# First SwiGLU with six hidden blocks at once and stationary weights in two parts; attention bias stored by 32 keys

## The chip, the cores and the metric

The program runs on one core of one Trainium2 chip. The metric is the device time of one execution in microseconds (us); lower is better. Beside a time there is the span of a profiled execution, which runs from its first to its last instruction and is a little shorter than the time. Five engines matter: PE (TensorE, matrix products), DVE (VectorE), ACT (ScalarE), POOL (GpSimd) and SP (SyncE, which here does nothing but issue transfers). On chip there are SBUF, 128 partitions wide, and PSUM, where PE accumulates. Weights come from DRAM by DMA.

## The reference

Two transformer layers on x of 256 tokens by D = 1024, all in fp32. A layer is: a SwiGLU, an attention, a second SwiGLU, each behind an RMS norm and a modulation by shift, scale and gate that are computed from a vector c.

```python
c_act = jax.nn.silu(c)
for layer in range(2):
    mods = c_act @ ada_w[layer] + ada_b[layer]
    sh1, sc1, g1, sh2, sc2, g2, sh3, sc3, g3 = jnp.split(mods, 9, axis=-1)
    h = modulate(rms_norm(x, norm_g[layer, 0]), sh1, sc1)       # h * (1 + scale) + shift
    x = x + 0.5 * g1 * swiglu(h, w_gate, w_up, w_down)          # (silu(h wg) * (h wu)) wd, F = 2816
    h = modulate(rms_norm(x, norm_g[layer, 1]), sh2, sc2)
    mix = moba_attention(h, ..., rel_bias, positions) if layer == 0 else mla_attention(h, ...)
    x = x + g2 * mix
    ...                                                         # second SwiGLU, as the first
```

The attention of layer 0 has 16 heads of 64 and adds to its scores a bias that depends on the distance of query and key: `bias_t[h, t5_bucket(qpos - kpos)]`, with 32 buckets, and minus a large number for keys that come after the query.

## The kernel before

**Products in parts.** Nearly all matrix products are made in a split form. An fp32 tile is rounded to a high part (ACT, line 623, `hi`) and the rest is its low part (DVE, line 624, `lo`); both are of a type that PE takes at a higher rate. `mm3` (lines 751 to 754) then adds up three products: high by high, low by high, high by low. `split_evac` (line 766) does the same to a result in PSUM, with `hh`/`hl` for activations.

**Order.** The program is written down in one order, and then a planner (`Order`, lines 238 on) lists all instructions of each engine anew. It costs every instruction with hand-set durations (`duration`, line 195), takes the PE order and the needs of later work as due times, and picks for each engine the most urgent one that is ready. `ranked(j)` gives the instructions of the first stage fixed ranks that override the due times; `hold` marks the bias and table work as side work that may not begin before the planned time `HELD`. Tiles come from rings of a fixed number of buffers, and a transfer into a buffer waits until the last reader of the tile before it is done. SP issues its transfers in order.

**The first SwiGLU.** It needs `h`, the normed and modulated x, before the modulation's vectors exist. So `first()` (line 1450) works through the eight slices `k` of 128 along D. For each slice: two column tiles `wt[k][0..1]` (128 x 1024) arrive, DVE multiplies each with c and sums along the row (`column`, line 634, one custom instruction and a short read of the accumulator), and `scale_col` (line 639) makes the scale out of it. x times 1/rms (line 1500, on ACT, with 1/rms from a small POOL operation, line 789) is transposed on PE (line 1502, "tr<-ident,y"). DVE makes z = xT * scale + shift (line 1510). Then come unsplit fp32 products: z is stationary, the 2 x 512 columns of the gate and up weights move (line 1514, two token tiles, four products a slice, 32 in all; in the trace one such product has two records). They make the first 512 of the 2816 hidden columns, with tokens along the partitions. z is split into the `hh`/`hl` that all later products use. The result, `accs`, goes through Silu (ACT) and a product (DVE, line 892), is transposed back (eight transposes of 128 x 128) and split.

**The rest of that SwiGLU** runs in pairs of blocks of 128 hidden columns (loop over `f0` in steps of 256, from line 905; "block n" is hidden columns 128n to 128n + 127). Here the weights are stationary and `h` moves: for each block 2 x 8 `mm3` of 256 columns (48 products), then the Silu (line 925, "g<-mm"), the product with the up part (line 926) and a split. The weights come as 1 MB loads of 128 x 2048 (`raw`, three buffers), and are split in two pieces of 1024. At the same time DVE works on the modulation vectors of later parts: columns as above, and accumulations (line 672, "acc<-adaw,cols,acc"), which "adaps" products (lines 682 and 683) sum up.

**The bias** is side work in the same loop. `bias_steps` (line 1078) makes comparisons on DVE (line 1149, "oh<-posq,key": 64 of them, in eight tiles `oh` of eight, four 256 wide and four 128 wide), and groups of 24 short bf16 products on PE (line 1128, "tr<-tab,oh", twelve groups), which turn the comparisons into bias values. After `k` of `HOOKS` of each block one group is put into the order, and all are in before `f0` = `SIDE_TO` * 256. ACT copies each group in four pieces into `bt` (line 1133; one tile of 128 x 2048 per pair of query tile and key tile). Two of the three `bt` are masked by a POOL affine select (line 1137), and all three are written to DRAM, `bias_d`, in four transfers each with 512 bytes in a run. The attention of layer 0 reads `bias_d` back in four groups of four heads on POOL's queue (line 1178, 6 KB in a run), and DVE adds it to the scores as it takes their minimum (line 989, "s<-at,bg"). `rope_tables` and `mla_consts` (among them line 1308, short products on DVE) are further side work, let in from `f0` = `ROPE_AT` * 256.

Of the kernel before, what the change touches and what calls it, by code (L numbers as in the profile page):

```python
# [21 lines left out]
P = 128  # L22
# [6 lines left out]
FB = 512  # L29
H = 16  # L30
DH = 64
GH = 4
# [22 lines left out]
SIDE_TO = 4  # L55
ROPE_AT = 7
# [29 lines left out]
def weight_tiles():  # L86


    for layer in range(2):
        for idx in range(2):  # L90
# [5 lines left out]
            for f0 in range(FB, F, S):  # L96
                for w in (wg, wu):
                    yield [(*w, f0)], 0, KD, S
# [27 lines left out]
def lay_out(v):  # L126
# [11 lines left out]
    out["first"] = np.stack([v["ffn_w_" + n][0, 0, :, :FB].reshape(KD, P, FB) for n in ("gate", "up")], axis=2)  # L138
# [23 lines left out]
    keys = pos.view(np.float32).reshape(NT, 4, 1, NB).repeat(NB, axis=2).reshape(NT, P, NB)  # L162
# [20 lines left out]
HELD = 34e3  # L183
# [334 lines left out]
def trunk(ctx: ExitStack, tc: tile.TileContext, a: dict, out: bass.AP):  # L518
# [351 lines left out]
    def ffn(layer, idx, h, after, ada_to, start=None):  # L870

        last = (layer, idx) == (1, 1)
        with ExitStack() as st:
            gp = st.enter_context(tc.tile_pool(name=nm("gp"), bufs=1))
            gT = {}
            accs = start() if start else {t: [] for t in range(NT)}
            ada_pace(ada_to, 90.0 if last else FFN_PACE)
            parts = [] if start else [[], []]
            for t in range(NT):
# [24 lines left out]
            gq = gp  # L904
            for f0 in range(FB, F, S):
# [8 lines left out]
                for f in range(f0 // P, (f0 + S) // P):  # L914
# [9 lines left out]
                    g = gp.tile([P, NT, P], F32, tag="gT", name=nm("g"), bufs=2)  # L924
                    nc.scalar.activation(g, ps[:, 0], AF.Silu)  # L925
                    nc.vector.tensor_tensor(g, ps[:, 1], g, op=ALU.mult)  # L926
                    gh, gl = [gq.tile([P, NT, P], F32R, tag=f"{nme}{f}", name=nm(nme)) for nme in ("gh", "gl")]
                    split_evac(gh, gl, g)
                    for t in range(NT):
                        gT[f, t] = gh[:, t, :], gl[:, t, :]  # L930
# [28 lines left out]
    def attention(ap, g, qTs, kTs, vs, bias, oT, state, after_s=None):  # L959
# [6 lines left out]
        def scores():  # L966
# [14 lines left out]
            for (t, es), ps3 in zip(UNITS, banks):  # L981
# [5 lines left out]
                else:  # L987
                    for i, e in enumerate(es):
                        nc.vector.tensor_tensor_reduce(s3[:, i, :], ps3[:, i, :], bias(t, e), 1.0, 3.0e38,
                                                       op0=ALU.add, op1=ALU.min, accum_out=mx[:, i:i + 1])  # L990
# [81 lines left out]
    bias_d = dp.tile([NG, P, GH * 3 * P], F32, name="bias_d")  # L1072
# [5 lines left out]
    def bias_steps():  # L1078
# [5 lines left out]
        with ExitStack() as st:  # L1084
# [35 lines left out]
            bt = {}  # L1120

            def mms(kb, t, c, oh):
                if c == 0:
                    bt[kb, t] = bp.tile([P, H, P], F32, tag="bt", name=nm("bt"), bufs=2)
# [6 lines left out]
                dst = bt[kb, t].rearrange("p h (j i) -> p h j i", j=4)  # L1131
                for j in range(4):
                    nc.scalar.activation(dst[:, :, j, 8 * c:8 * c + 8],
                         pt.rearrange("p (i j h) -> p j h i", i=8, j=4)[:, j], AF.Copy)
                if c == 3:
                    if t == kb:
                        nc.gpsimd.affine_select(bt[kb, t], bt[kb, t], pattern=[[0, H], [-1, P]],
                                                compare_op=ALU.is_ge, fill=-NEG, base=0, channel_multiplier=1)
                    for g in range(NG):
                        nc.sync.dma_start(  # L1140
                            bias_d[g].rearrange("p (h k) -> p h k", h=GH)[:, :, (t + kb) * P:(t + kb + 1) * P],
                            bt[kb, t][:, g * GH:(g + 1) * GH, :])

            for kb in range(NT):
                n = P * (NT - kb)
                for c in range(4):
                    oh = bp.tile([P, 8, n], BF16, tag="oh", name=nm("oh"), bufs=2)
# [26 lines left out]
    def moba(h, after):  # L1174
        with ExitStack() as st:
            ap = st.enter_context(tc.tile_pool(name="moba", bufs=1))
            bg = {0: ap.tile([P, GH, 3 * P], F32, tag="bg", name=nm("bg"))}
            nc.gpsimd.dma_start(bg[0].rearrange("p h k -> p (h k)"), bias_d[0])
# [42 lines left out]
            def to_T(g):  # L1221
# [16 lines left out]
                def load_bias():  # L1238
                    if g + 1 < NG:
                        bg[g + 1] = ap.tile([P, GH, 3 * P], F32, tag="bg", name=nm("bg"))  # L1240
# [108 lines left out]
    def mla(h, hs, after):  # L1349
        with ExitStack() as st:  # L1350
# [96 lines left out]
            out_proj(oT, (1, 1), after)  # L1447


    def first():  # L1450


        key = (0, 0)
# [113 lines left out]
```

## Time and profile before

| | before |
|---|---|
| time, median of 3 runs | 1019.33 us (1019.13 to 1019.91) |
| time of the profiled execution | 1019.3 us |
| its span | 1017.5 us |
| granted TensorE clock, mean | 1.000 |
| read from DRAM, written | 255.34 MB, 4.19 MB |
| unsplit products of the first stage, busy time up to 106 us | 23.1 us in 48 records and 7.1 us in 16 |
| high parts on ACT (all) | 325.5 us in 316, mean 1041 ns |
| low parts on DVE (all) | 375.2 us in 316, mean 1201 ns |
| copies of the bias on ACT | 9.3 us in 48, mean 298 ns |

How to read the profile's lines. The first part of the page gives for each engine its busy time, the share of the span and the number of instructions; PEld is the loading of stationary tiles, which overlaps PE. Products are pipelined: one that is listed with 0.28 us may have another start 0.12 us after it. A line of the timeline gives start and duration in us, engine, line of the code, operation, tiles (out<-in), shape and type, "xN" for N in a row put together, and in brackets the idle time ahead of it with what ended it. A table of windows has one row for each stretch of time: its length, and then for each engine the busy time with the number of instructions. The chain of waits is followed back from the last instruction: at each step to what released it.

### The profile page before, as it was taken

What the parts mean: (1) busy time and instruction counts of PE and PEld (TensorE: products, weight loads), DVE (VectorE), ACT (ScalarE), POOL (GpSimd) and SP (SyncE); (2) the same over time, 40 slices, a digit from 0 to 9 for tenths busy, and PEclk for the clock granted to TensorE, in tenths of its full rate; (3) what the DMA queues carried; (4) which work ended last, traced back from release to release, by engine and by line L of the source; (5) the groups of instructions that cost most, each with busy time, mean ns of one, the idle gap of its engine ahead of it and who ended that gap; (6) DMA issues with size and microseconds to landing.
All of it is one profiled execution on the core that took longest, in us unless ns stands there. A gap on an engine that the chain in (4) does not pass through costs nothing.

```text
span 1017.5 us, 16904 instructions
## 1 busy us (share of the span) xinstructions
PE 1000.0 (98%) x6538; PEld 885.5 (87%) x6538; DVE 805.9 (79%) x1310; ACT 566.7 (56%) x1008; POOL 76.7 (8%) x118
## 2 busy tenths in 40 slices
PE   7999999999999999999999999999999999999998
PEld 3598998888888799999888999988888889999986
DVE  7999888799989899888889986544998789555542
ACT  4354544368757774455357445543779785455421
POOL 2011000012231000000000000000143010000000
PEclk9999999999999999999999999999999999999999
DMA  9969999889885689988988995463343467544530
GB/s 361 412 227 341 324 338 325 307 302 345 293 327 189 244 302 369 325 316 309 350 313 319 342 333 179 166 227 106 104 138 131 173 229 276 200 167 166 211 141 21
DMA packets 56578, 260.63 MB, mean 256 GB/s; under 512 B 6065, under 2 KB 12721, under 8 KB 38066
## 3 DMA queue, kind: packets, MB, share of 16 engines
q1 hardware_dynamic: 55442, 256.05, 69.6%
q0 software_dynamic: 768, 3.17, 0.9%
q8 instruction: 51, 0.84, 0.3%
q10 hardware_dynamic: 288, 0.33, 0.2%
q14 instruction: 29, 0.24, 0.1%
HBM read 255.34 MB, written 4.19 MB: 255 GB/s over the span
## 4 chain that ended last, share of the span: by engine, by line
PE 88%; DVE 7%; DMA 3%; ACT 1%; issue 1%; POOL 0%; SPq 0%; ACTq 0%; DVEq 0%
PE mm L752 26%; PE mm L754 26%; PE mm L753 26%; PE mm L1514 2%; PE at L976 2%; DVE oh L1149 1%; DVE lo L624 1%; PE at L1031 1%; DMA btab<-in_tab_dram 1%; PE at L1011 1%; PE tr L802 1%; DVE acc L672 1%; DMA bias_d<-bt 1%; DMA raw<-in_w_dram 1%; DMA x<-in_x_dram 0%
## 5 line engine op out<-in xcount | busy, mean ns | idle before, releaser
L624 DVE TENSOR_TENSOR lo<-raw,hi 128x1024 fp32r<-128x1024 f32 (+2 forms) x316 | 375.2, 1201 | 117.6 <-ACT hi L623 117.1
L623 ACT ACTIVATE hi<-raw 128x1024 fp32r<-128x1024 f32 (+2 forms) x316 | 325.5, 1041 | 174.3 <-PE mm L754 121.9
L752 PE MATMUL mm<-hh,hi 128*128 128x256 f32 x1152 | 323.6, 284 | 0.7 <-ACT hi L623 0.7
L754 PE MATMUL mm<-hh,lo 128*128 128x256 f32 x1152 | 322.9, 283 | 0.7 <-DVE lo L624 0.7
L753 PE MATMUL mm<-hl,hi 128*128 128x256 f32 x1152 | 322.9, 283 | 0.0
L752 PEld LDWEIGHTS mm<-hh,hi 128*128 128x128 f32 x1152 | 219.3, 192 | 1.9 <-ACT hi L623 0.9
L754 PEld LDWEIGHTS mm<-hh,lo 128*128 128x128 f32 x1152 | 219.7, 192 | 1.4 <-DVE lo L624 0.9
L753 PEld LDWEIGHTS mm<-hl,hi 128*128 128x128 f32 x1152 | 220.0, 192 | 0.9 <-issue 0.2
L634 DVE CUSTOM_DVE_ANT_0 adaw<-adaw,c_b,cols 128x1024 f32<-128x1024 f32 x112 | 141.3, 1282 | 3.3 <-DMA adaw<-in_ada_dram 2.9
L752 PE MATMUL mm<-hi,gh 128*128 128x512 f32 x352 | 137.1, 390 | 0.0
L753 PE MATMUL mm<-lo,gh 128*128 128x512 f32 x352 | 136.8, 389 | 0.0
L754 PE MATMUL mm<-hi,gl 128*128 128x512 f32 x352 | 136.6, 389 | 0.0
L925 ACT ACTIVATE g<-mm 128x256 f32<-128x256 f32 x72 | 27.6, 383 | 139.2 <-PE mm L754 123.8
L752 PE MATMUL mm<-hi,hh 128*128 128x512 f32 (+1 forms) x240 | 95.2, 402 | 0.6 <-ACT hh L767 0.5
L754 PE MATMUL mm<-hi,hl 128*128 128x512 f32 (+1 forms) x240 | 92.5, 392 | 1.6 <-DVE hl L768 1.6
L753 PE MATMUL mm<-lo,hh 128*128 128x512 f32 (+1 forms) x240 | 93.3, 393 | 0.0
L754 PEld LDWEIGHTS mm<-hi,gl 128*128 128x128 f32 x352 | 66.1, 188 | 13.7
L753 PEld LDWEIGHTS mm<-lo,gh 128*128 128x128 f32 x352 | 66.1, 188 | 13.3
L752 PEld LDWEIGHTS mm<-hi,gh 128*128 128x128 f32 x352 | 66.1, 188 | 13.2
L672 DVE SCALAR_TENSOR_TENSOR acc<-adaw,cols,acc 128x1024 f32<-128x1024 f32 x48 | 61.3, 1278 | 0.1
L926 DVE TENSOR_TENSOR g<-mm,g 128x256 f32<-128x256 f32 x72 | 30.3, 421 | 34.9 <-ACT g L925 34.7
L754 PEld LDWEIGHTS mm<-hi,hl 128*128 128x128 f32 x240 | 45.1, 188 | 10.5 <-DVE hl L768 2.1
(204 smaller groups left out, 1081.8 us busy)
## 6 DMA issues: line engine op xcount, KB each, us to landing
raw<-in_w_dram SPq DMA_DIRECT2D x144, 1024.0 KB, 6.2
adaw<-in_ada_dram SPq DMA_DIRECT2D x160, 512.0 KB, 6.3
raw<-in_w_dram SPq DMA_DIRECT2D x12, 512.0 KB, 3.7
raw<-in_w_dram SPq DMA_DIRECT2D x6, 576.0 KB, 3.6
raw<-in_first_dram SPq DMA_DIRECT2D x6, 512.0 KB, 10.2
bias_d<-bt SPq DMA_DIRECT2D x12, 256.0 KB, 5.6
bg<-bias_d POOLq DMA_DIRECT2D x4, 768.0 KB, 5.6
raw<-in_w_dram SPq DMA_DIRECT2D x2, 768.0 KB, 4.3
```

What stands on the lines that cost most here:

```text
L623: nc.scalar.activation(hi, src, AF.Copy)
L624: nc.vector.tensor_tensor(lo, src, hi.bitcast(F32), op=ALU.subtract)
L634: nc.vector.tensor_tensor_reduce(wt, wt, c_b, 1.0, cols[:, i, c:c + 1], op0=ALU.mult, op1=ALU.add, accum_out=m_cols[:, i, c:c + 1])
L672: nc.vector.scalar_tensor_tensor(acc, ada_tile(j, k), cact[:, k:k + 1], acc, op0=ALU.mult, op1=ALU.add)
L752: nc.tensor.matmul(ps, lh, rh, start=start, stop=False)
L753: nc.tensor.matmul(ps, lh, rl, start=False, stop=False)
L754: nc.tensor.matmul(ps, ll, rh, start=False, stop=stop)
L802: nc.tensor.transpose(kslice(pt, j), kslice(y, j), ident)
L925: nc.scalar.activation(g, ps[:, 0], AF.Silu)
L926: nc.vector.tensor_tensor(g, ps[:, 1], g, op=ALU.mult)
L976: nc.tensor.matmul(ps3[:, i, :], qTs(e, t), kTs(e, nk), start=bias is not None, stop=bias is not None or i == len(es) - 1)
L1514: nc.tensor.matmul(accs[t][i], kslice(z, t), w1[k][:, i * FB:(i + 1) * FB], start=k == 0, stop=k == KD - 1)
```

## The change

Eight things are changed, all in the first SwiGLU and in the bias of layer 0's attention.

- `first` makes six blocks (`B1` = 6, 768 hidden columns) in place of the first four. The weights are now stationary, in high and low parts, and `h` moves, as in the rest of the loop: 8 slices x 6 blocks x 2 matrices x 3 products of 256 columns. All six blocks accumulate side by side in six PSUM banks, each with gate and up in one bank. So no result needs transposing, and each goes through `units`, the code that the other blocks use. The loop over `f0` starts at 768.
- Since two accumulations share a bank, each bank is first cleared by products with a tile of zeros (nine of them, bf16, 512 columns, before any data is there).
- x is transposed by a product with a diagonal matrix that holds 1/rms: x is stationary, `diag[t]` moves (16 fp32 products). This replaces the scaling on ACT, the transposes and the copy of `xT` to SBUF. Ten short products with zeros follow those of slice 1.
- z is made on ACT, from PSUM, and no longer on DVE.
- The weights of a slice are 128 x 1536: the high parts in three ACT copies of 512; of the low part, DVE and POOL do one half each (512 + 256 columns and 256 + 512) for slices 0 to 5, and DVE does all of it for slices 6 and 7.
- These weights come in 24 transfers of 256 KB (with six slices' worth of buffers, three of `raw` and three of `adaw`), in place of eight of 512 KB.
- The bias is kept by 32 keys: each group of 24 products gives one `bt` tile (128 x 16 heads x 32 keys), by one ACT copy; eight of the twelve are masked, by an affine select of 512 each; each is written by one transfer with 2 KB in a run. It is read back with 512 bytes in a run, and DVE reads scores and bias with a four-dimensional pattern. The order of the keys in the table of key positions is changed accordingly. `oh` has three buffers, `bt` three.
- `SIDE_TO` goes from 4 to 6, `ROPE_AT` from 7 to 9, `HELD` from 34e3 to 40e3 (planned ns).

The core of the diff:

```diff
-SIDE_TO = 4
-ROPE_AT = 7
+B1 = 6
+SIDE_TO = 6
+ROPE_AT = 9
...
-HELD = 34e3
+HELD = 40e3
...
-    out["first"] = np.stack([v["ffn_w_" + n][0, 0, :, :FB].reshape(KD, P, FB) for n in ("gate", "up")], axis=2)
+    out["first"] = np.stack([v["ffn_w_" + n][0, 0, :, :B1 * P].reshape(KD, P, B1, P) for n in ("gate", "up")], axis=3)
+    out["first"] = out["first"].reshape(KD, P, 3, -1).transpose(0, 2, 1, 3)
...
+            def units(f, ps):
+                g = gp.tile([P, NT, P], F32, tag="gT", name=nm("g"), bufs=2)
+                nc.scalar.activation(g, ps[:, 0], AF.Silu)
+                nc.vector.tensor_tensor(g, ps[:, 1], g, op=ALU.mult)
+                gh, gl = [gq.tile([P, NT, P], F32R, tag=f"{nme}{f}", name=nm(nme)) for nme in ("gh", "gl")]
+                split_evac(gh, gl, g)
...
-            for f0 in range(FB, F, S):
+            for f0 in range(B1 * P if start else FB, F, S):
...
-    bias_d = dp.tile([NG, P, GH * 3 * P], F32, name="bias_d")
+    bias_d = dp.tile([3, P // NB, P, H * NB], F32, name="bias_d")
...
-                dst = bt[kb, t].rearrange("p h (j i) -> p h j i", j=4)
-                for j in range(4):
-                    nc.scalar.activation(dst[:, :, j, 8 * c:8 * c + 8],
-                         pt.rearrange("p (i j h) -> p j h i", i=8, j=4)[:, j], AF.Copy)
-                if c == 3:
-                    if t == kb:
-                        nc.gpsimd.affine_select(bt[kb, t], bt[kb, t], pattern=[[0, H], [-1, P]],
-                                                compare_op=ALU.is_ge, fill=-NEG, base=0, channel_multiplier=1)
-                    for g in range(NG):
-                        nc.sync.dma_start(
-                            bias_d[g].rearrange("p (h k) -> p h k", h=GH)[:, :, (t + kb) * P:(t + kb + 1) * P],
-                            bt[kb, t][:, g * GH:(g + 1) * GH, :])
+                bt = bp.tile([P, H, NB], F32, tag="bt", name=nm("bt"), bufs=3)
+                nc.scalar.activation(bt, pt.rearrange("p (m h) -> p h m", h=H), AF.Copy)
+                if t == kb:
+                    nc.gpsimd.affine_select(bt, bt, pattern=[[0, H], [-1, NB]], compare_op=ALU.is_ge, fill=-NEG,
+                                            base=-NB * c, channel_multiplier=1)
+                nc.sync.dma_start(bias_d[t + kb, c], bt.rearrange("p h k -> p (h k)"))
...
+            def load_bias(g):
+                bg[g] = ap.tile([P, 3, P // NB, GH * NB], F32, tag="bg", name=nm("bg"))
+                cs = slice(g * GH * NB, (g + 1) * GH * NB)
+                nc.gpsimd.dma_start(bg[g], bias_d[:, :, :, cs].rearrange("u c p f -> p u c f"))
...
+            for f in (*range(B1), *range(3)):
+                nc.tensor.matmul(accs[f], zeros[:, :P], zeros, start=f not in cleared, stop=False)
+                cleared.add(f)
...
+                    diag.append(fp.tile([P, P], F32, name=nm("diag")))
+                    nc.scalar.activation(diag[t], ident, AF.Copy, scale=rstd_of(t))
...
+            def transposed(k):
+                xT = ps_x[k % 2][:, :S]
+                with ranked(2 * k + 1):
+                    for t in range(NT):
+                        nc.tensor.matmul(kslice(xT, t), kslice(xs[t], k), diag[t], start=True, stop=k != 1 or t == 0)
+                    for i in range(fill if k == 1 else 0):
+                        nc.tensor.matmul(kslice(xT, 1), zeros[:, :P], zeros[:, :P], start=False, stop=i == fill - 1)
+                return xT
...
                     for i in range(2):
                         column(key, i, k, wt[k][i])
                     scale_col(key, k, 1)
                     z = tp.tile([P, S], F32, tag="y", name=nm("z"), bufs=4)
-                nc.vector.tensor_scalar(z, xT[k // 4][:, k % 4 * S:(k % 4 + 1) * S], col_slice(1, key, k, 1), col_slice(0, key, k, 1),
-                                        op0=ALU.mult, op1=ALU.add)
+                    nc.scalar.activation(z, xT[k], AF.Identity, scale=key, k, 1), bias=col_slice(0, key, k, 1))
...
-                for i in range(2):
-                    nc.tensor.matmul(accs[t][i], kslice(z, t), w1[k][:, i * FB:(i + 1) * FB],
-                                     start=k == 0, stop=k == KD - 1)
+                    hi, lo = [fp.tile([P, n1], F32R, tag=g, name=nm(g), bufs=2) for g in ("whi", "wlo")]
+                    for j in range(3):
+                        cs = slice(j * third, (j + 1) * third)
+                        nc.scalar.activation(hi[:, cs], w1(k, j), AF.Copy)
+                        cut = (0, third // 2, third)[j] if k < KD - 2 else 0
+                        for on, c0, c1 in ((nc.vector, 0, third - cut), (nc.gpsimd, third - cut, third)):
+                            if c0 < c1:
+                                on.tensor_tensor(lo[:, j * third + c0:j * third + c1], w1(k, j)[:, c0:c1],
+                                                 hi.bitcast(F32)[:, j * third + c0:j * third + c1], op=ALU.subtract)
...
+                for f in range(B1):
+                    for i in range(2):
+                        c = (2 * f + i) * P
+                        ps, wh, wl = accs[f][:, i], hi[:, c:c + P], lo[:, c:c + P]
+                        nc.tensor.matmul(ps, wh, hh, start=False, stop=False)
+                        nc.tensor.matmul(ps, wh, hl, start=False, stop=False)
+                        nc.tensor.matmul(ps, wl, hh, start=False, stop=i == 1 and k == KD - 1)
...
+            for f in range(B1):
+                units(f, accs[f])
```

168 lines of the change are left out of this document (84 added, 84 removed).

## The prediction

> **What bounds the kernel now.** I read the page's busy table and chain first, then the windows of the first 120 us, since everything the change touches ends there or (the bias) is read by 330 us.
>
> ```profile
> PE 1000.0 (98%) x6538; PEld 885.5 (87%) x6538; DVE 805.9 (79%) x1310; ACT 566.7 (56%) x1008; POOL 76.7 (8%) x118
> ...
> PE 88%; DVE 7%; DMA 3%; ACT 1%; issue 1%; POOL 0%; SPq 0%; ACTq 0%; DVEq 0%
> ...
> 20.00:30.00 10.00, 10.00 (x24) 4.37 (x23) 9.01 (x17) 0.84 (x2) 0.00 (x0) 1.00 1.03 410
> ...
> 60.00:80.00 20.00, 18.97 (x292) 18.23 (x291) 20.00 (x52) 9.83 (x30) 3.60 (x1) 1.00 0.76 249
> 80.00:100.00 20.00, 18.40 (x167) 17.66 (x166) 19.80 (x33) 11.43 (x29) 3.84 (x3) 1.00 1.04 347
> 100.00:120.00 20.00, 20.00 (x167) 19.91 (x166) 17.58 (x28) 10.83 (x18) 0.00 (x0) 1.00 0.95 352
> ```
>
> The columns are PE, PEld, DVE, ACT, POOL, clock, DMA share, GB/s. PE bounds the whole, but between 60 and 100 us DVE is full (20.00 and 19.80 of 20) and PE is not. Before that DMA is full (1.03). So the early stage has three limits in turn, and a gain of PE time there counts only if DVE follows. From 100 us PE is full and DVE has 12% spare: what PE has gained by then stays gained.
>
> The stage on PE, in order of time:
>
> ```profile
> 10.32 1.97 PE L1502 MATMUL tr<-ident,y 128*128 128x128 f32 x8 [0.28 <-ACT y L1500]
> ...
> 13.63 23.06 PE L1514 MATMUL mm<-raw,z 128*128 128x512 f32 x48
> 36.88 7.11 PE L1514 MATMUL mm<-w,z 128*128 128x512 f32 x16 [0.18 <-DMA w<-in_first_dram]
> ...
> 43.94 0.28 PE L753 MATMUL mm<-hl,hi 128*128 128x256 f32 x1
> 44.06 0.28 PE L754 MATMUL mm<-hh,lo 128*128 128x256 f32 x1
> ...
> 55.48 0.87 PE L1128 MATMUL tr<-tab,oh 128*128 128x64 bf16 x24
> 56.19 0.36 PE L752 MATMUL mm<-hh,hi 128*128 128x256 f32 x1
> ...
> 97.18 0.39 PE L682 MATMUL adaps<-hi,ones_r 128*128 128x512 f32 x1
> 97.41 0.40 PE L683 MATMUL adaps<-lo,ones_r 128*128 128x512 f32 x1
> ...
> 106.19 0.39 ACT L925 ACTIVATE g<-mm 128x256 f32<-128x256 f32 x1 [0.59 <-PE mm L754]
> ```
>
> The f32 matmuls hold PE from 13.63 to 43.4 us. After that a split matmul of 256 columns starts every 0.12 us, and a bias group of 24 costs 0.71 us. My milestone is the last row: the Silu of block 11 (the first 1536 of the 2816 hidden columns and all bias groups done), at 106.2 us.
>
> **The change on PE.** Removed: the f32 matmuls (29.8 us as they ran), 96 split matmuls of blocks 4 and 5 (11.5), eight transposes. Added: 6 blocks x 2 matrices x 3 x 8 = 288 split matmuls, 288 x 0.12 = 34.6 us, and 16 products with the diagonal. Nothing like the latter stands in the trace; the transposes above cost 1.97/8 = 0.25 us, an f32 512-column record about 23.06/48 = 0.48, so 0.12 to 0.25; I take 0.25, of which 12 fall after the start: 3 us. The nine clearing matmuls resemble the 0.23 us of the adaps rows, lie ahead of the first data, and cost the path 0 to 0.5. Starting at 13.6 as now, PE alone would finish six blocks at 51.2 and, with 6 x 48 x 0.12 = 34.6 and 12 groups of 0.79 (0.71 and a slower restart), reach the milestone at 95.3. The four adaps matmuls (0.9 us), now ahead of it, come later in the changed order, so like stands against 105.3: PE alone gains about 10 us.
>
> **The change on DVE.** DVE's own costs, from rows that follow one another without a gap:
>
> ```profile
> 8.21 1.28 DVE L634 CUSTOM_DVE_ANT_0 adaw<-adaw,c_b,cols 128x1024 f32<-128x1024 f32 x1 [0.36 <-ACT y L1500]
> ...
> 16.26 1.28 DVE L634 CUSTOM_DVE_ANT_0 adaw<-adaw,c_b,cols 128x1024 f32<-128x1024 f32 x1 [0.52 <-DMA adaw<-in_ada_dram]
> 18.75 0.15 DVE L639 SCALAR_TENSOR_TENSOR m_cols<-m_cols,cols 128x1 f32<-128x1 f32 x1
> ...
> 20.10 1.28 DVE L634 CUSTOM_DVE_ANT_0 adaw<-adaw,c_b,cols 128x1024 f32<-128x1024 f32 x1 [0.34 <-DMA adaw<-in_ada_dram]
> ...
> 42.77 0.68 DVE L892 TENSOR_TENSOR g<-mm,g 128x512 f32<-128x512 f32 x1
> 43.37 1.22 DVE L624 TENSOR_TENSOR lo<-raw,hi 128x1024 fp32r<-128x1024 f32 x1
> ...
> 62.71 2.19 DVE L1149 TENSOR_SCALAR oh<-posq,key 128x256 bf16<-128x256 f32 x8
> 64.81 1.22 DVE L624 TENSOR_TENSOR lo<-raw,hi 128x1024 fp32r<-128x1024 f32 x1
> 65.94 0.42 DVE L926 TENSOR_TENSOR g<-mm,g 128x256 f32<-128x256 f32 x1
> 66.28 1.22 DVE L624 TENSOR_TENSOR lo<-raw,hi 128x1024 fp32r<-128x1024 f32 x1
> 67.41 1.66 DVE L1149 TENSOR_SCALAR oh<-posq,key 128x128 bf16<-128x128 f32 x8
> 68.98 0.42 DVE L926 TENSOR_TENSOR g<-mm,g 128x256 f32<-128x256 f32 x1
> 69.31 1.28 DVE L672 SCALAR_TENSOR_TENSOR acc<-adaw,cols,acc 128x1024 f32<-128x1024 f32 x1
> 70.51 1.22 DVE L624 TENSOR_TENSOR lo<-raw,hi 128x1024 fp32r<-128x1024 f32 x1
> 71.64 2.00 DVE L1308 TENSOR_TENSOR sink<-rw_sin,cols 128x16 f32<-128x16 f32 x1
> 73.57 1.65 DVE L1149 TENSOR_SCALAR oh<-posq,key 128x128 bf16<-128x128 f32 x8
> ...
> 86.00 1.98 DVE L1308 TENSOR_TENSOR sink<-rw_sin,cols 128x16 f32<-128x16 f32 x1
> 87.91 0.16 DVE L1308 TENSOR_TENSOR cosq<-rw_cos,cols 128x16 f32<-128x16 f32 x1
> ```
>
> From start to start: two columns 2.49 us, with the scaling 2.64; a difference over 512 columns 0.60, over 1024 1.13, over 256 0.34; a comparison 0.26 (256 wide) or 0.20 (128); an accumulation 1.20. In the first stage the changed DVE does 8 x 2.64 = 21.1, eight low parts of z 2.7, and low parts of the weights: 6 x (0.60 + 0.34) for k below 6, and 6 x 0.60 for the last two, 9.2. Sum 33.0; the z products go to ACT, which is busy 56%. Beginning at 8.2 as now, with some 1.5 us of waits (the second pair of columns waits for its load, low parts of z wait for ACT, both estimated), it would end at 42.7. DMA does not hold that up: the pairs now come 3.84 us apart for 1.5 MB, so 4.5 us for 1.75 MB.
>
> But POOL now does the other 768 low columns of each k below 6, and here is the crux:
>
> ```profile
> 70.02 3.60 POOL L1137 TENSOR_SCALAR_AFFINE_SELECT bt<-bt 128x2048 f32<-128x2048 f32 x1 [57.85 <-ACT bt L1133]
> ...
> 85.61 2.34 POOL L1137 TENSOR_SCALAR_AFFINE_SELECT bt<-bt 128x2048 f32<-128x2048 f32 x1 [11.99 <-DMA bias_d<-bt]
> ```
>
> Both times a 16-element DVE product beside it took 2.00 and 1.98 us in place of 0.16, until POOL's end; the first select had itself waited through two DVE instructions. They exclude each other, and POOL holds DVE about 1.85 us for 2048 elements, 0.9 ns each. A subtraction on POOL is not in the trace. It reads two operands: at one stream's price 768 elements hold DVE 0.69 us, at two 1.38. I take the middle, 1.1, and DVE ends the stage at 42.7 + 6 x 1.1 = 49.3 (46.8 to 51.0).
>
> After that, up to the last of the 64 comparisons, the changed order gives DVE 14 low parts of 1024 (15.8), 32 + 32 comparisons (8.3 + 6.4), 7 accumulations (8.4), 17 pieces of 256 (5.8) and some 36 small ones of about 0.1 (3.6): 48.3. Eight affine selects of 512 replace the two of 2048; seven precede that point, holding DVE 7 x 0.46 = 3.2 (0 if each falls beside work it does not exclude). So 49.3 + 48.3 + 3.2 = 100.8. PE, which would be there at 95, waits: its last bias products and the end of block 11 follow, about 0.9 us: milestone 101.7. Against 105.3 that is **3.6 us gained**. At the two ends of POOL's price 6.1 and 1.9.
>
> [...]
>
> **Parts that cost nothing if the cover holds.**
>
> ```profile
> bias_d<-bt SPq DMA_DIRECT2D x12, 256.0 KB, 5.6
> bg<-bias_d POOLq DMA_DIRECT2D x4, 768.0 KB, 5.6
> L989 DVE CUSTOM_DVE_ANT_0 s<-at,bg x32: 283/354/425, 254.4 to 323.1; 128x128 f32<-128x128 f32 x16, 128x256 f32<-128x256 f32 x16
> L1178 POOL DMA_DIRECT2D bg<-bias_d x1: 587/587/587, 226.4 to 226.4; - x1
> ```
>
> The bias leaves in 2 KB rows in place of 512 B ones and is read back in 512 B pieces (now 6 KB ones). The first read is issued at 226.4 and used at 254.4; it lands in 5.6 us, so it may take five times as long. Without that cover each microsecond is one of DVE and soon of PE. One ACT copy in place of four sits off the path. First-stage loads go out as 24 of 256 KB in place of 8 of 512 KB on SP; the wait that counts there is for the buffers of weights 6 and 7 (read by POOL and DVE at k = 0, long before). The first weights of block 6 sit in the third buffer, free after k = 3; those behind wait for DVE's last low parts and have 5.8 us (48 matmuls) of cover, and the bias table queued behind them on SP is first used, by the changed order, some 13 us later.
>
> **The rivals.**
>
> (a) DVE is not held: columns and POOL run side by side, PE sets the milestone at 95.5. For it: PE's sum, and the clock of 1.00. Against: two 2 us stalls, and that low parts and columns, like the stalled products, read two tiles. Gain 9.8: 1009.5.
>
> (b) POOL's subtraction is dearer than two streams, and the change is slower. At three streams (two reads, a write) the hold is 2.08 us; with a fixed half microsecond for each of POOL's two instructions, 3.1. It decides from 1.7 us a k, where 6 x 0.6 eats the 3.6. At 2.08 the loss is 2.3 (1021.6), at 3.1 8.4 (1027.7); I put it at 1023.5. For it: every unknown of the sum lies on this side, and the planner, which orders the code by hand-set costs, knows no exclusion. Against: POOL's rows show nothing beyond one stream.
>
> The Trainium skill's "GPSIMD Engine Reference" (Performance versus the Vector engine) gives an fp32 subtraction 2.6 cycles of 1.2 GHz an element, a hold of an estimated 1.66 us a k; by that figure the sum comes out near 1019, on this rival's threshold.
>
> (c) The gain is given back. At the milestone DVE has one tile of weights and two columns less done than now (about 7 us), and 100 to 120 us shows 2.4 us of slack in 20. If a low part comes late there, 1019.
>
> **How the numbers follow.** Forecast 0.42, (a) 0.16, (b) 0.30, (c) 0.12. The profiled execution's span is 1017.5 and its time 1019.3, 1.8 around it, as the median 1019.33: 1019.3 - 3.6 = **1015.7**; its own range 1013.2 to 1017.4. The whole range, 1009 to 1025.5, takes in (a) and most of (b). 0.2% is 2.0 us, about what a measurement tells from no change. Faster: three quarters of the forecast (0.32) and (a), 0.48; same 0.24 (the rest of the forecast, (c), a little of (b)); slower 0.28, most of (b).
>
> **What would show it.** Right: block 11's Silu near 101.7; DVE without gaps from 13 to 100 us; columns or low parts of weights stretched while POOL subtracts, about 1.1 us a k; PE waiting for DVE's comparisons. Wrong: PE back to back from 13.6 to 51 (then (a)); POOL instructions above 1.7 us a k with DVE stalled behind them (then (b)); or a milestone near 102 with PE idle after 105 (then (c)). A bias read that DVE waits for would break the cover.

## The result, and the profile after

The changed kernel takes 1023.79 us (median of 5 runs, 1022.45 to 1024.05) against 1019.33 us (five runs, 1019.06 to 1019.91): a ratio of 1.0041, interval 1.0026 to 1.0055. It is 4.5 us slower; 3.6 us faster was forecast. The span of its profiled execution is 1022.0 us, also 4.5 over the 1017.5 of before.

The page of the changed kernel, its busy table and its chain:

```profile
PE 1004.7 (98%) x6693; PEld 902.3 (88%) x6693; DVE 814.9 (80%) x1321; ACT 572.9 (56%) x991; POOL 101.9 (10%) x136
...
PE 85%; DVE 8%; DMA 5%; ACT 1%; issue 0%; POOL 0%; SPq 0%; DVEq 0%; ACTq 0%
```

POOL is busy for 25 us more, DVE for 9, and PE has 3 points less of the chain. The windows of the first 120 us, in the columns of the prediction's (PE, PEld, DVE, ACT, POOL, clock, DMA share, GB/s), show where:

```profile
20.00:30.00 10.00, 9.60 (x76) 8.98 (x74) 8.95 (x15) 3.90 (x8) 4.67 (x3) 1.00 1.03 398
30.00:40.00 10.00, 8.91 (x68) 8.13 (x67) 9.76 (x13) 3.85 (x8) 7.05 (x4) 1.00 1.03 399
40.00:50.00 10.00, 7.61 (x56) 6.64 (x54) 9.42 (x18) 4.06 (x9) 6.78 (x22) 1.00 0.93 365
50.00:60.00 10.00, 9.45 (x66) 9.45 (x67) 8.79 (x22) 6.18 (x12) 0.00 (x0) 0.83 0.59 206
60.00:80.00 20.00, 19.83 (x218) 18.91 (x218) 19.05 (x61) 12.75 (x23) 2.75 (x34) 1.00 0.68 224
80.00:100.00 20.00, 18.68 (x273) 17.78 (x270) 18.43 (x45) 8.59 (x15) 3.64 (x4) 1.00 0.76 254
100.00:120.00 20.00, 19.84 (x183) 18.96 (x182) 20.00 (x31) 11.21 (x17) 4.07 (x5) 1.00 0.94 326
```

In the first stage PE is now the engine with gaps (7.61 of 10 between 40 and 50 us), and right behind them the granted clock is 0.83 in place of 1.00. One slice of the stage on DVE, and then its end:

```profile
24.27 0.43 DVE L1548 TENSOR_TENSOR wlo<-raw,whi 128x256 fp32r<-128x256 f32 x1
24.61 1.76 DVE L636 CUSTOM_DVE_ANT_0 adaw<-adaw,c_b,cols 128x1024 f32<-128x1024 f32 x1
26.31 0.08 DVE L636 DVE_READ_ACCUMULATOR2_ANT m_cols<- 128x1 f32 x1
26.31 2.30 DVE L636 CUSTOM_DVE_ANT_0 adaw<-adaw,c_b,cols 128x1024 f32<-128x1024 f32 x1
28.54 0.08 DVE L636 DVE_READ_ACCUMULATOR2_ANT m_cols<- 128x1 f32 x1
28.54 0.15 DVE L641 SCALAR_TENSOR_TENSOR m_cols<-m_cols,cols 128x1 f32<-128x1 f32 x1
28.61 0.68 DVE L1548 TENSOR_TENSOR wlo<-raw,whi 128x512 fp32r<-128x512 f32 x1
29.77 0.43 DVE L770 TENSOR_TENSOR hl<-z,hh 128x256 fp32r<-128x256 f32 x1 [0.48 <-ACT hh L769]
...
47.42 0.83 DVE L770 TENSOR_TENSOR hl<-z,hh 128x256 fp32r<-128x256 f32 x1
48.18 1.63 DVE L636 CUSTOM_DVE_ANT_0 adaw<-adaw,c_b,cols 128x1024 f32<-128x1024 f32 x1
...
51.63 2.48 DVE L1548 TENSOR_TENSOR wlo<-raw,whi 128x512 fp32r<-128x512 f32 x4
```

And POOL beside it:

```profile
24.37 3.16 POOL L1548 TENSOR_TENSOR wlo<-raw,whi 128x256 fp32r<-128x256 f32 x2 [2.86 <-ACT whi L1544]
...
46.54 2.21 POOL L1317 TENSOR_SCALAR_AFFINE_SELECT mask<-mask 128x512 bf16<-128x512 bf16 x2
```

A column that takes 1.28 us alone takes 1.76 beside POOL's subtraction of 256 columns (0.48 more) and 2.30 beside that of 512 (1.03 more): 1.5 us a slice, 2.0 ns an element. Over slices 0 to 5 the stretched rows add up to 9.2 us. Three times in the stage DVE is then idle for 0.48 us until ACT has made z and its high part, since too little work of its own is left to fill that time. Near the stage's end POOL's masks for the last attention, which before were made at 11 us, hold a low part of z (0.83 in place of 0.42) and a column (1.63).

PE, listed with what ended its gaps:

```profile
35.90 0.71 PE L1523 MATMUL tr<-diag,x 128*128 128x128 f32 x4 [0.84 <-ACT z L1535]
...
47.97 0.39 PE L1557 MATMUL mm<-hh,whi 128*128 128x256 f32 x1 [1.33 <-ACT whi L1544]
...
50.55 0.38 PE L1559 MATMUL mm<-hh,wlo 128*128 128x256 f32 x1 [1.50 <-DVE wlo L1548]
```

So DVE's last low parts of the stage end at 54.1 us (the four that start at 51.63), where the prediction had 49.3.

### The profile page after: what moved, and what is told of

Same layout as the page of the kernel before. It is cut to its first block, busy times and chain, and to the rows that moved or that the text cites. A ratio compares the mean times of both kernels' runs of the same rounds, so it can differ in the third digit from the quotient of the medians.

```text
span 1022.0 us, 17281 instructions
## 1 busy us (share of the span) xinstructions
PE 1004.7 (98%) x6693; PEld 902.3 (88%) x6693; DVE 814.9 (80%) x1321; ACT 572.9 (56%) x991; POOL 101.9 (10%) x136
## 4 chain that ended last, share of the span: by engine, by line
PE 85%; DVE 8%; DMA 5%; ACT 1%; issue 0%; POOL 0%; SPq 0%; DVEq 0%; ACTq 0%
PE mm L754 26%; PE mm L755 26%; PE mm L756 26%; DMA adaw<-in_ada_dram 3%; PE at L985 2%; DVE lo L626 2%; DMA raw<-in_first_dram 2%; PE at L1041 1%; DVE oh L1150 1%; PE at L1021 1%; DMA raw<-in_w_dram 1%; PE tr L804 1%; DVE acc L674 1%; DVE z L820 0%; PE tr L1409 0%
## 5 line engine op out<-in xcount | busy, mean ns | idle before, releaser
L626 DVE TENSOR_TENSOR lo<-raw,hi 128x1024 fp32r<-128x1024 f32 (+3 forms) x312 | 370.3, 1199 | 118.6 <-ACT hi L625 118.3
L625 ACT ACTIVATE hi<-raw 128x1024 fp32r<-128x1024 f32 (+3 forms) x312 | 321.6, 1040 | 173.6 <-PE mm L756 120.4
L756 PE MATMUL mm<-hh,lo 128*128 128x256 f32 x1120 | 315.0, 284 | 0.0
L755 PE MATMUL mm<-hl,hi 128*128 128x256 f32 x1120 | 314.5, 284 | 0.0
L754 PE MATMUL mm<-hh,hi 128*128 128x256 f32 x1120 | 313.3, 284 | 0.2 <-ACT hi L625 0.2
L756 PEld LDWEIGHTS mm<-hh,lo 128*128 128x128 f32 x1120 | 213.9, 192 | 0.7
L755 PEld LDWEIGHTS mm<-hl,hi 128*128 128x128 f32 x1120 | 214.0, 192 | 0.6
L754 PEld LDWEIGHTS mm<-hh,hi 128*128 128x128 f32 x1120 | 213.0, 192 | 1.1 <-ACT hi L625 0.4
L636 DVE CUSTOM_DVE_ANT_0 adaw<-adaw,c_b,cols 128x1024 f32<-128x1024 f32 x112 | 148.4, 1349 | 1.2 <-ACT c_b L1495 1.2
L756 PEld LDWEIGHTS mm<-hi,hl 128*128 128x128 f32 x240 | 45.1, 188 | 10.3 <-DVE hl L770 2.1
```

The costliest lines, as they stand in the source:

```text
L625: nc.scalar.activation(hi, src, AF.Copy)
L626: nc.vector.tensor_tensor(lo, src, hi.bitcast(F32), op=ALU.subtract)
L636: nc.vector.tensor_tensor_reduce(wt, wt, c_b, 1.0, cols[:, i, c:c + 1], op0=ALU.mult, op1=ALU.add, accum_out=m_cols[:, i, c:c + 1])
L754: nc.tensor.matmul(ps, lh, rh, start=start, stop=False)
L755: nc.tensor.matmul(ps, lh, rl, start=False, stop=False)
L756: nc.tensor.matmul(ps, ll, rh, start=False, stop=stop)
```

## The experiments

Each kernel was timed in alternation with the kernel before, whose median lay between 1019.3 and 1019.5 us in these runs. Line numbers in the profile's rows are those of the kernel of the run.

| run | median, us | ratio to before, interval |
|---|---|---|
| the change | 1023.79 | 1.0041 (1.0026 to 1.0055) |
| all low parts on DVE | 1013.52 | 0.9946 (0.9934 to 0.9958) |
| the same, and POOL subtracts for nobody | 1023.09 | 1.0036 (1.0024 to 1.0048) |
| before with the bias part alone | 1019.04 | 0.9997 (0.9988 to 1.0006) |
| the change without the bias part | 1025.6 | 1.0060 (1.0044 to 1.0075) |
| 256 columns on POOL | 1014.87 | 0.9952 (0.9938 to 0.9966) |
| the change, PE's gaps filled | 1021.62 | 1.0020 (1.0011 to 1.0029) |
| the change, masks early | 1021.77 | 1.0010 (0.9991 to 1.0029) |
| all on DVE, PE warmed earlier | 1013.65 | 0.9938 (0.9925 to 0.9951) |
| all on DVE, POOL writes zeros | 1015.77 | 0.9964 (0.9950 to 0.9977) |
| all on DVE, POOL selects | 1016.97 | 0.9977 (0.9967 to 0.9986) |
| the change, gaps filled and masks early | 1020.81 | 1.0016 (1.0008 to 1.0025) |
| all on DVE, three y buffers | 1015.20 | 0.9958 (0.9944 to 0.9972) |

### POOL's share of the low parts

```diff
-                        cut = (0, third // 2, third)[j] if k < KD - 2 else 0
+                        cut = 0
```

> The changed kernel with all low parts of the first weights on DVE, none on POOL. Theory 1 (POOL's subtraction holds DVE): in the changed kernel's trace the holds in slices 0 to 5 add up to 9.2 us, 1.53 a slice, and DVE itself would need 0.94 a slice for those 768 columns (0.60 + 0.34). So 6 x 0.6 = 3.6 us come back: about 1020.2, columns at 1.28 us throughout. Rival A (POOL relieves DVE, the loss is elsewhere): 6 x 0.94 = 5.6 us more, about 1029. Rival B (the loss lies behind the first stage): 1023.8, unchanged.

1013.52 us: 10.3 less than the change, 5.8 less than the kernel before, and the fastest measured here together with one other. Theory 1 holds in its direction and both rivals fall, but it gave a third of the gain. The same slice on DVE in this run, all columns at 1.28 and no wait for ACT, since a low part of 512 stands in that place now:

```profile
24.36 1.28 DVE L636 CUSTOM_DVE_ANT_0 adaw<-adaw,c_b,cols 128x1024 f32<-128x1024 f32 x1
...
25.57 1.28 DVE L636 CUSTOM_DVE_ANT_0 adaw<-adaw,c_b,cols 128x1024 f32<-128x1024 f32 x1
...
26.77 0.16 DVE L641 SCALAR_TENSOR_TENSOR m_cols<-m_cols,cols 128x1 f32<-128x1 f32 x1
26.84 1.29 DVE L1548 TENSOR_TENSOR wlo<-raw,whi 128x512 fp32r<-128x512 f32 x2
28.05 0.42 DVE L770 TENSOR_TENSOR hl<-z,hh 128x256 fp32r<-128x256 f32 x1
28.38 0.69 DVE L1548 TENSOR_TENSOR wlo<-raw,whi 128x512 fp32r<-128x512 f32 x1
28.98 1.28 DVE L636 CUSTOM_DVE_ANT_0 adaw<-adaw,c_b,cols 128x1024 f32<-128x1024 f32 x1
```

From column to column the slice takes 28.98 - 24.36 = 4.62 us; in the change the slice from 24.61 to 30.63 took 6.02. DVE does more and is done 1.4 us sooner. The stage ends on DVE at 48.8 us in place of 54.1, and the last of the 64 comparisons at 99.7 in place of 109.5: nearly all of the gain is there by then. The windows from 30 us on have no gap of PE left in the stage, and the clock stays whole:

```profile
30.00:40.00 10.00, 10.00 (x87) 10.00 (x86) 9.94 (x21) 5.09 (x10) 0.00 (x0) 1.00 1.03 400
40.00:50.00 10.00, 10.00 (x86) 10.00 (x86) 9.21 (x20) 7.38 (x13) 0.00 (x0) 1.00 1.02 390
50.00:60.00 10.00, 10.00 (x86) 10.00 (x85) 10.00 (x21) 6.79 (x14) 1.12 (x32) 1.00 0.92 358
```

With that line the planner also put POOL's masks back to 11 us. There they hold DVE no less than in the change: a scaling takes 0.59 in place of 0.15 and a pair of low parts 1.70 in place of 1.28, together 0.86 us against 0.78. But that is early in the stage, and what the move is worth within the 10.3 us, this run does not show apart. First POOL, then DVE:

```profile
11.28 2.24 POOL L1317 TENSOR_SCALAR_AFFINE_SELECT mask<-mask 128x512 bf16<-128x512 bf16 x2
```

```profile
11.85 0.59 DVE L641 SCALAR_TENSOR_TENSOR m_cols<-m_cols,cols 128x1 f32<-128x1 f32 x1
12.36 1.70 DVE L1548 TENSOR_TENSOR wlo<-raw,whi 128x512 fp32r<-128x512 f32 x2
```

The next run puts the subtraction back without its use; `spare` has no reader, and DVE makes the whole low part.

```diff
+                        nc.vector.tensor_tensor(lo[:, cs], w1(k, j), hi.bitcast(F32)[:, cs], op=ALU.subtract)
+                        for p0 in range(third - ((0, third // 2, third)[j] if k < KD - 2 else 0), third, 256):
+                            spare = fp.tile([P, 256], F32, tag="spare", name=nm("spare"), bufs=1)
+                            nc.gpsimd.tensor_tensor(spare, w1(k, j)[:, p0:p0 + 256],
+                                                    hi.bitcast(F32)[:, j * third + p0:j * third + p0 + 256], op=ALU.subtract)
```

> As the run before with all low parts on DVE, but POOL in addition makes its former share (768 columns of slices 0 to 5, in pieces of 256) into a spare tile that nobody reads; the ring of y tiles has three buffers for the space. Theory 1: the hold is paid without the help, 9.2 us over the run before, about 1029. Rival A: POOL's work costs DVE nothing, the time of the run before. The difference between the two runs, over 6 x 768 elements, is the price of POOL's subtraction to this kernel.

1023.09 us, 9.6 over the run before. Its DVE rows show two columns and a scaling stretched in each of slices 3 to 5, by 0.48, 0.48 and 0.53 us (slice 4 is shown); in slices 0 to 2 it is other rows of DVE, low parts among them, by as much in sum:

```profile
33.16 1.76 DVE L636 CUSTOM_DVE_ANT_0 adaw<-adaw,c_b,cols 128x1024 f32<-128x1024 f32 x1
...
34.85 1.76 DVE L636 CUSTOM_DVE_ANT_0 adaw<-adaw,c_b,cols 128x1024 f32<-128x1024 f32 x1
...
36.54 0.68 DVE L641 SCALAR_TENSOR_TENSOR m_cols<-m_cols,cols 128x1 f32<-128x1 f32 x1
```

What POOL does with two tiles costs the kernel nearly what it holds, whether or not it is of use. A part of the 9.6 turned out not to be POOL's: the three y buffers, which made the space for `spare`, cost something far behind. The control has three y buffers and no work of POOL:

```diff
-                    z = tp.tile([P, S], F32, tag="y", name=nm("z"), bufs=4)
+                    z = tp.tile([P, S], F32, tag="y", name=nm("z"), bufs=3)
```

(so at all three places of the ring, and `cut = 0`)

> All low parts on DVE, with three buffers in the ring of y tiles and nothing on POOL: the kernel against which the runs with work of POOL nobody reads have to be held. In the trace of the run with the memsets the late instructions stand 1.3 us ahead of the run with four buffers until 630 us and 0.6 behind at the end: 1.9 us are lost between 630 and 840 us, far behind the first stage. If the ring is what costs them: 1015.4 (1013.5 + 1.9), and the memsets cost nothing. Rival D: the ring costs nothing, 1013.5, and the 2.2 us of the run with the memsets are POOL's.

1015.20 us. By the medians the ring costs 1.7 (the intervals of the two ratios overlap; the traces, in the last section, show the loss itself), and the subtraction nobody reads 1023.09 - 1015.20 = 7.9 us, against 9.2 us of holds. In the traces of these two runs the same instructions of DVE stand 8.3 us apart from 80 us on and 8.4 at the end, so the price is paid in the first stage.

### Which work of POOL holds DVE

```diff
+                            nc.gpsimd.memset(w1(k, j)[:, p0:p0 + 256], 0.0)
```

> All low parts on DVE (1013.5), and POOL in addition writes zeros over 768 columns of each of slices 0 to 5, in pieces of 256 and after their last readers, without reading anything. Theory 1 says that what holds DVE are POOL's reads: 1013.5, no stretched column. Rival D (any work of POOL in SBUF holds DVE): the first memset of 128 x 1024 took 0.95 us, 0.93 ns an element, so 768 x 0.93 = 0.71 us a slice and 6 x 0.71 = 4.3 us more, 1017.8.

1015.77 us, 0.6 over the control with three y buffers and inside the spread of its own runs (1014.88 to 1016.76). The memsets fall beside low parts, and these keep their durations. First POOL, then DVE, in this run:

```profile
31.94 0.31 POOL L1547 MEMSET raw<- 128x256 f32 x1 [4.33 <-DVE wlo L1545]
32.54 0.56 POOL L1547 MEMSET raw<- 128x256 f32 x2 [0.29 <-DVE wlo L1545]
```

```profile
31.19 1.28 DVE L1545 TENSOR_TENSOR wlo<-raw,whi 128x512 fp32r<-128x512 f32 x2
32.40 0.42 DVE L770 TENSOR_TENSOR hl<-z,hh 128x256 fp32r<-128x256 f32 x1
32.73 0.68 DVE L1545 TENSOR_TENSOR wlo<-raw,whi 128x512 fp32r<-128x512 f32 x1
```

1.28, 0.42 and 0.68 us are what the same operations take with POOL idle, so rival D falls. The Trainium skill ("SBUF — State Buffer", Who interferes with whom) has it that DVE with two inputs in SBUF is shut out by a POOL instruction that reads SBUF and not by one that only writes; this pair of runs agrees, with 7.9 and 0.6 us.

```diff
+                            nc.gpsimd.affine_select(spare, w1(k, j)[:, p0:p0 + 256], pattern=[[-1, 256]],
+                                                    compare_op=ALU.is_ge, fill=0.0, base=0, channel_multiplier=1)
```

> All low parts on DVE, and POOL in addition makes an affine select of the same 768 columns of slices 0 to 5 into the spare tile: one tile read in place of two. Theory 1 with a price for each tile read: 0.9 ns an element, 0.69 us a slice, 6 x 0.69 = 4.1 us over 1013.5, 1017.6, against 9.6 us for the subtraction. Rival E (POOL holds DVE for the length of its work, whatever it reads): about the 1023.1 of the run with the subtraction.

1016.97 us, 1.8 over the control with three buffers, so rival E falls. In the trace a slice is held about 0.5 us (a column 1.40, a scaling 0.34, a pair of low parts 1.48 in place of 1.29), a third of the subtraction's and not half:

```profile
30.92 1.40 DVE L636 CUSTOM_DVE_ANT_0 adaw<-adaw,c_b,cols 128x1024 f32<-128x1024 f32 x1
...
32.26 0.34 DVE L641 SCALAR_TENSOR_TENSOR m_cols<-m_cols,cols 128x1 f32<-128x1 f32 x1
32.52 1.48 DVE L1545 TENSOR_TENSOR wlo<-raw,whi 128x512 fp32r<-128x512 f32 x2
```

The two runs differ in the kind of POOL's instruction as well as in the tiles that it reads. That the price goes with the tiles read fits both and the memset, but is not shown apart.

### How the loss grows with POOL's share

```diff
+                        cut = third // 2 if j == 1 and k < KD - 2 else 0
```

> The changed kernel with 256 of the 1536 low columns of slices 0 to 5 on POOL (768 in the change, none in the run with all on DVE, 1013.5). Theory 1, by holds alone: 256 columns hold DVE 0.48 us (so in the trace of the run with the spare tile) and save it 0.34, so 6 x 0.14 = 0.8 us over 1013.5: 1014.3. Theory 2 (the loss grows with what the hold does further on: DVE's idle time behind ACT, PE's gaps and the half clock after them): no gaps of PE yet, so also under 1015.5. Rival, a loss in proportion to POOL's share: 1013.5 + 10.3/3 = 1016.9.

1014.87 us, 1.35 over none on POOL. A third of the share costs an eighth of the loss, so the loss is not in proportion. In the trace the holds add up to 3.0 us, and DVE is spared 6 x 0.34 = 2.0, so they explain about 1.0 of the 1.35. PE is not free of gaps here (the longest are 0.86 us, for a high part by ACT, and 0.44), but its clock stays at 1.00 from 10 us on. That the larger share is dearer because PE's longer gaps there are followed by a slower clock is theory 2; these two points fit it and do not prove it.

### PE's gaps and the clock behind them

```diff
+                        idle = 14 if k == KD - 2 and f == i == 0 else 0
+                        for _ in range(idle):
+                            nc.tensor.matmul(ps, zeros[:, :P], zeros[:, :S], start=False, stop=False)
...
+                        for _ in range(idle):
+                            nc.tensor.matmul(ps, zeros[:, :P], zeros[:, :S], start=False, stop=False)
```

> The changed kernel with 2 x 14 short products with zeros put into PE's order at slice 6, where its trace has gaps of 1.49 and 1.66 us and, from 51.1 us on, 3.41 us of half the granted clock. Theory 2 (PE's gaps cost twice, by the half clock behind them): the clock stays at 1.00 and 3.41 / 2 = 1.7 us come back, 1022.1. Rival: DVE is what is waited for then, too, and the time stays at 1023.8.

1021.62 us: 2.2 less than the change, for 28 products that add nothing. The stage ends on DVE as before, at 53.9 us, but the clock stays, and DVE, which behind the stage sat idle in the change (0.47, 0.52, 0.35 and 0.60 us between 56.7 and 61.6 us, for results of PE and what ACT and POOL make of them), is full. Its window, to be held against the 0.83 and the 8.79 of DVE above:

```profile
50.00:60.00 10.00, 9.45 (x77) 9.23 (x77) 9.79 (x22) 5.91 (x11) 0.96 (x29) 1.00 0.65 222
```

The edit also gave DVE another order behind the stage: three accumulations stand at 57.55, 59.08 and 60.94 us, where the change has its first at 63.38. At the last Silu of this SwiGLU the run is only 0.6 us ahead of the change (168.33 against 168.90), and the whole 2.2 us only from 360 us on. So the run shows that gaps filled keep the clock, and 2.2 us for both together; how much of that is the clock's and how much the new order's stays open.

```diff
+    with ranked(0):
+        for t in range(NT):
+            m4 = masks[t].rearrange("p (e k) -> p e k", k=P * (t + 1))
+            nc.gpsimd.memset(masks[t], 0.0)
+            nc.gpsimd.affine_select(m4, m4, pattern=[[0, 4 // (t + 1)], [-1, P * (t + 1)]],
+                                    compare_op=ALU.is_ge, fill=NEG, base=t * P, channel_multiplier=1)
```

> The changed kernel with POOL's two masks for the last attention made at the very start in place of 45.6 to 48.7 us. In the changed kernel's trace they hold DVE 0.8 us there (0.42 at a low part of z, 0.36 at a column) in a stretch in which PE waits for both: theory 1 expects 0.8 us back, 1023.0, and somewhat more if PE's gap there gets short enough for the clock to stay. Rival: nothing, 1023.8.

1021.77 us, 2.0 less than the change, where 0.8 was expected; its runs lie between 1020.10 and 1023.82, so the size is uncertain. The second gap of PE falls from 1.50 to 0.79 us. The clock dropped all the same in its profiled execution (0.95 and 0.88 in the windows from 40 to 60 us, in sum as much as the 1.00 and 0.83 of the change), so the clock is not what the 1.2 us beyond the hold came from; that stays open. The profiled execution itself is 1.3 us shorter than that of the change.

> The changed kernel with both the zero products in PE's gaps and the early masks. Alone they brought 2.2 and 2.0 us of the 10.3 that moving POOL's share to DVE brings. Theory 2: both shorten or fill the same gap of PE, so together less than their sum, 1020.5 to 1021.5, and the rest, 7 us or more, is the hold itself. Rival: they add up, 1019.6.

1020.81 us: 3.0 for the two together, between 2.2 and the sum of 4.2, as theory 2 had it. The accumulations moved here as well (the first at 56.76 us). 7.3 of the 10.3 us remain with POOL's share.

```diff
-                        nc.tensor.matmul(kslice(xT, t), kslice(xs[t], k), diag[t], start=True, stop=k != 1 or t == 0)
+                        early = 16 if k == t == 0 else 0
+                        nc.tensor.matmul(kslice(xT, t), kslice(xs[t], k), diag[t], start=True,
+                                         stop=not early and (k != 1 or t == 0))
+                        for i in range(early):
+                            nc.tensor.matmul(kslice(xT, t), zeros[:, :P], zeros[:, :P], start=False, stop=i == early - 1)
```

(and `fill` 16 in place of 10)

> All low parts on DVE (1013.5), and 22 more short products with zeros where PE waits for x (16 between the two token tiles of slice 0, six more after slice 1). In the profile of the run with all low parts on DVE the granted clock is a half from 8.7 to 18.9 us, and the split products begin at 14.0, so that up to 4.9 us of PE's work runs at half: theory 2 expects up to 2.4 us less where the clock comes earlier, 1011 to 1013.5. Rival: DVE sets the pace there, 1013.5.

1013.65 us, no gain, though its clock is at 1.00 from 10 us on. With all on DVE the stage goes at DVE's pace, and a PE at half the clock keeps up with it for those 5 us: a miss for theory 2, which had priced the half clock without asking who is waited for.

### The two parts of the change

> The kernel before with the bias part of the change alone (32 keys a tile, one copy, eight selects of 512, 2 KB rows out, 512 B pieces back). Theory 1 says that the loss is in the first stage: 1019.3, within 1 us. Rival C (the bias costs): 1021 or more, with DVE waiting at the addition of the bias or held longer by the selects.

1019.04 us: the new form of the bias costs and brings nothing that can be measured.

> The changed kernel with the bias as it was before (the ring of y tiles has three buffers for the space). Theory 1: the loss stays, 1023.8 within 1 us. Rival C: it goes, 1019 to 1020.

1025.6 us, with runs from 1022.66 to 1028.12, and some 1.7 us of it by the control are those of the y ring. The loss is in the first stage; rival C falls both times.

## Why the prediction was wrong

The step that failed is the price of POOL's subtraction and what it leads to: "I take the middle, 1.1, and DVE ends the stage at 42.7 + 6 x 1.1 = 49.3", and behind it a sum for DVE without any wait. The mechanism of the hold was the right one, and rival (b) named it; its size was not, and three terms stood at nothing.

**The hold.** 1.5 us a slice, by the stretched rows, and not 1.1. The upper end of "at two [streams] 1.38" was too low as well: two tiles read cost 2.0 ns an element, more than twice the 0.9 of a select. That is 6 x 0.43 = 2.6 us, and puts the forecast at 1018.3. The hold is under the 1.7 from which rival (b) decided, so by the sum it would not have made the change slower. That rival (b)'s 1023.5 lies 0.3 us from the measured time is therefore luck. The estimate by the Trainium skill's figure ("GPSIMD Engine Reference", Performance versus the Vector engine), 1.66 us, was closer than the middle of the prediction's two rows.

**The other terms of the stage.** DVE's work itself was sized right: of the 45.2 us from its first column at 8.89 to 54.1, 9.2 are the hold, 0.8 POOL's masks and 2.3 waits, which leaves 33.0, as forecast. The masks stood at nothing: at 11 us in the kernel before, they moved into the stage's end. The waits are 2.3 in place of "some 1.5" (0.48 three times for ACT's chain, and smaller ones). And DVE began at 8.89, not at 8.2. The clearing products, said to "cost the path 0 to 0.5", hold PE until 4.45 us in the change:

```profile
1.35 3.17 PE L1503 MATMUL mm<-zeros 128*128 128x512 bf16 x7 [1.35 <-DVE zeros L1461]
```

The products that spread c over the partitions, for which DVE's first column waits, start there at 4.45 in place of 3.38. Hold 2.6, masks 0.8, waits 0.8 and start 0.7 make up the 4.8 by which the stage ended late, 54.1 against 49.3.

**What stands behind the stage.** The sum gave DVE 48.3 + 3.2 = 51.5 us up to the last comparison and took PE's waiting as free ("PE, which would be there at 95, waits"). In the trace DVE is busy for 51.7 us there, as forecast, but takes 55.4, since it is idle for 3.7. Two gaps of PE, of 1.33 and 1.50 us, were followed by 3.4 us at half the clock, and DVE then waited in turn, 1.9 us by 61.6. A wait of 1.57 us follows at 90 us, which in the kernel before has no counterpart: ACT's high part waited 4.15 us for a load of weights. In the trace of the change:

```profile
89.73 1.06 ACT L625 ACTIVATE hi<-raw 128x1024 fp32r<-128x1024 f32 x1 [4.15 <-DMA raw<-in_w_dram]
```

```profile
91.58 0.42 DVE L884 TENSOR_TENSOR g<-mm,g 128x256 f32<-128x256 f32 x1 [1.57 <-ACT g L883]
```

SP issued that load at 81.62 us, right behind three writes of the bias that it had begun at 77.01; whether they held it up, no run shows. The run with all low parts on DVE has a like wait, 1.12 us at 83.3, so it is not POOL's subtraction alone that makes it.

**The account.** The last comparison ends at 109.5 us, where the sum had 100.8: 4.8 us late at the stage's end and 3.9 behind it, 8.7 in all, beside the 8.1 by which the time missed the forecast. These terms are read off one trace. What runs took away is POOL's share (10.3 us) and the gaps and masks (3.0 together, where DVE's wait at 90 us is gone too); the other terms were not taken away alone.

**The milestone** was badly chosen. Block 11's Silu comes at 119.35 us in the change, 13 us after that of before, because PE's changed order works on blocks 12 and 13 ahead of it; these follow at 121.2 and 123.0. Like for like is the last Silu of this SwiGLU, 163.80 us before and 168.90 after: 5.1 later, of which 4.5 are left at the end.

**The selects of the bias** were priced at 0.46 each where they hold DVE. Five of the seven do, by 0.47 to 0.54, and two find nothing to hold: 2.5 us in place of 3.2. A row of six comparisons beside a select took 2.11 us, where six need 6 x 0.26 + 0.08 = 1.64. In the trace of the change, POOL and then DVE:

```profile
76.44 1.54 POOL L1141 TENSOR_SCALAR_AFFINE_SELECT bt<-bt 128x512 f32<-128x512 f32 x1 [14.92 <-ACT bt L1139]
```

```profile
77.33 2.11 DVE L1150 TENSOR_SCALAR oh<-posq,key 128x256 bf16<-128x256 f32 x6
```

The comparisons have one input in SBUF and are held all the same. From 128 elements to 256 they grow by 0.06 us (0.20 to 0.26), 0.5 ns an element and twice as fast as a subtraction. The Trainium skill ("SBUF — State Buffer", Who interferes with whom) says that an instruction of DVE in a two-port mode shuts POOL out and is shut out by it. Their rate fits such a mode; no run here shows the mode itself.

**What held.** The split products at 0.12 us; the product with the diagonal at 0.23 (0.25 taken); the cover of the bias: its read lands in 7.1 us in place of 5.6, issued at 230.9 and used at 259.1.

```profile
bg<-bias_d POOLq DMA_DIRECT2D x4, 768.0 KB, 7.1
```

Something late at the milestone, as rival (c) had it, did come with that load, as one term of several. Rival (a), PE alone, was 9.8 us of gain; without POOL's share the kernel reaches 5.8 of them.

## What to carry to other kernels

Work given to POOL was not free for DVE here: price it by what it takes from DVE (2.0 ns an element for a subtraction of two tiles, 0.7 for a select of one, nothing that could be measured for a memset) and give it only if that is less than what DVE would need itself (1.04 ns for the subtraction). Try the smallest form first, all on one engine: it was 10.3 us faster than the shared one. A slowed engine's waits can turn into gaps of the next one. A gap of PE can be followed by a slower clock, and filling it brought something only where PE was waited for (2.2 us in the change, with another order of DVE's work; nothing where DVE set the pace).

## What the runs showed of the hardware

The granted clock fell to a half for the 3.4 us that follow PE's two gaps, and came back whole. Three windows of the change, over the gaps, the half clock and the time behind it, show it:

```profile
46.00:51.00 5.00, 2.17 (x14) 1.60 (x13) 5.00 (x11) 3.00 (x7) 2.74 (x4) 1.00 0.63 252
51.20:54.50 3.30, 3.30 (x17) 3.30 (x17) 3.24 (x9) 2.84 (x5) 0.00 (x0) 0.50 0.24 37
54.60:58.00 3.40, 3.40 (x30) 3.40 (x30) 2.40 (x7) 1.22 (x2) 0.00 (x0) 1.00 0.96 352
```

PE was busy 2.17 of 5 us ahead of it, started 17 products in the 3.3 us at half and 30 in the 3.4 us behind. 28 small products in the gaps kept the clock whole; shortening one gap to 0.79 us did not.

One buffer less in the ring of y tiles, with all else equal, cost 1.7 us by the medians. In the traces of the two kernels with all low parts on DVE, the late instructions stand 1.8 us earlier with three buffers until 718 us and 0.2 later from 844 us to the end, so 2.0 us are lost between, far behind the first stage.
